# GLA q and k projections of heads 2 and 3: q with tokens stationary, k in two token halves

## Chip, cores and metric

The kernel runs on one core of a Trainium2 chip. The metric is device microseconds (us) of one execution, and lower is better. The core has a matrix engine (TensorE, "PE" in the profile, with its weight loads as "PEld"), three engines for elementwise work (VectorE "DVE", ScalarE "ACT", GpSimd "POOL") and SyncE ("SP"), which here only issues DMAs. Every engine works through its own instruction list in order and waits where an operand is not ready.

## The reference

One layer of a hybrid decoder for 320 tokens: 256 of a prompt and 8 sequences of 8 sample tokens, all with the same weights. What matters here is the input projection and the GLA branch:

```python
h = _rmsnorm(x, norm_mix_w)
proj = h @ _f32(w_in)
mq, mk, mv, mo, mi, mf, gq, gk, gv, gr, gal, gate_a, gate_b = jnp.split(proj, split_at, axis=-1)
...
q_g = gq.reshape(B, T, G_HEADS, G_DK) * (G_DK ** -0.5)
k_g = gk.reshape(B, T, G_HEADS, G_DK)
...
o_g, S1 = _gla(q_g, k_g, v_g, log_a, _f32(S0))
```

`G_HEADS` is 4 and `G_DK` is 128, so q and k of one GLA head are 128 columns of `w_in` each; `D_MODEL`, the length of the contraction, is 2048. An mLSTM branch of four heads, a merge with gates and a ConvFFN follow.

## The kernel before

**Precision and layout.** Each float32 product is made of three matmuls in a reduced float32 format (`F32R`): the weight is split into a high and a low part (`wh`, `wl`), the normalized input as well (`hH[k]`, `hL[k]` for the 16 blocks `k` of 128 of the contraction), and `mm3` (L75 to L78) adds high x high, high x low and low x high into one accumulator. In `mm3` a 128x128 block of weights is stationary and all 320 tokens move, so the result stands with output columns on partitions and tokens along the free axis.

**Weights.** `weights` (L63 to L73) loads 512 KB into a tile `raw`, rounds it on ACT into `wh` (L71) and subtracts on DVE into `wl` (L72). `raw` has four buffers; `wh` and `wl` have three each. A buffer of `wh` or `wl` is free again when the last matmul that reads it is done, so at most three chunks of weights are split ahead of PE or held by it.

**Projections.** `product` (L89) accumulates 256 output columns in two PSUM tiles `big` (96 matmuls). `proj2` uses it for v, and for q, k and v of the mLSTM heads. `proj1` (L442) makes 128 columns in one `big` tile with 48 matmuls, and is used for q and k of GLA heads 2 and 3, whose columns are projected when those heads come up (heads 0 and 1 are done at the start). PSUM is two pools of four banks, `big` and `mx`; the small matmuls of the heads use `mx`.

**Heads.** The loop over `h` at L789 issues for each head: q and k (heads 2 and 3), v, `gla_head`, then q, k and v of the mLSTM head and `mlstm_head`. Both head functions are long chains of small steps over PE, DVE, ACT and POOL. They share the tiles `vH`, `vL`, `vs` (the split values), so a head's chain starts when the chain before it has used them. Their recurrent states lie in a pool of three buffers with the tag `state`, handed out in turn: `S0` of the GLA head (L581), then two tiles `C0` of the mLSTM head (L701). A buffer can be written again when the stores of its last user (L695 for `S0`, L787 for `C0`) have landed.

**Order of work.** The program is written head by head, and a scheduler moves each engine's instructions so that the chains of a head lie between the dense projection matmuls of what comes next. What it decides is fixed in each engine's list before the run. The chain of GLA head 1 thus lies, on PE, among the projections of head 2.

Lines that the prediction's steps touch, in the order of a GLA head: levels of the attention matrix (L626, L634, L643), split of it (L507, L508, L496, L498), numerators (L513, L500), norm (L528 to L539), transposes (L543), `hn` (L545, L546), decayed keys (L658 to L664), transposes (L669, L670), their split (L673, L674, L558, L560), masked keys `km` (L684), state update (L689 on PE, L693 on DVE), store of the state (L695). Of the mLSTM head: values (L476, L466, L483, L480), product with the state (L574), scores (L755 to L757), numerators (L513 again).

Of the kernel before, what the change touches and what calls it, by code (L numbers as in the profile page):

```python
# [10 lines left out]
F32 = mybir.dt.float32  # L11
F32R = mybir.dt.float32r
U8 = mybir.dt.uint8
AF = mybir.ActivationFunctionType
ALU = mybir.AluOpType
PSUM = bass.MemoryType.PSUM

P = 128
DM = 2048
NK = DM // P  # L20
T = 256
B = 8
S = 8
NS = B * S
N = T + NS
H = 4
DH = 256
DK = 128
DV = 256
# [8 lines left out]
C_GQ, C_GK, C_GV, C_GR = 4104, 4616, 5128, 6152  # L38
# [5 lines left out]
def step_kernel(ctx: ExitStack, tc: tile.TileContext, a: dict):  # L44
    nc = tc.nc
    cp = ctx.enter_context(tc.tile_pool(name="cp", bufs=1))
# [4 lines left out]
    def big():  # L51
        return ps.tile([P, 512], F32, tag="big", name="big")

    def mx(name="mx"):
        return ps.tile([P, 512], F32, tag="mx", name=name)
# [4 lines left out]
    w_in = a["w_in"][0]  # L60


    def weights(src, kc, mc, halves=1):  # L63

        raw = ring.tile([P, kc, mc * P], F32, tag="raw", name="raw", bufs=RAW)
        nc.sync.dma_start(raw, src.rearrange("(k p) c -> p k c", p=P))
        hi = ring.tile([P, kc, mc * P], F32R, tag="wh", name="wh", bufs=3)
        lo = ring.tile([P, kc, mc * P], F32R, tag="wl", name="wl", bufs=3)
        for i in range(halves):
            ks = slice(i * kc // halves, (i + 1) * kc // halves)  # L70
            nc.scalar.activation(hi[:, ks], raw[:, ks], AF.Copy)  # L71
            nc.vector.tensor_tensor(lo[:, ks], raw[:, ks], hi[:, ks].bitcast(F32), op=ALU.subtract)  # L72
        return hi, lo  # L73

    def mm3(out, wh, wl, xh, xl, first, last):  # L75
        nc.tensor.matmul(out, wh, xh, start=first, stop=False)  # L76
        nc.tensor.matmul(out, wh, xl, start=False, stop=False)  # L77
        nc.tensor.matmul(out, wl, xh, start=False, stop=last)  # L78
# [18 lines left out]
    ident = cp.tile([P, P], F32, name="ident")  # L97
# [20 lines left out]
    rstd_bc = cp.tile([P, N], F32, name="rstd_bc")  # L118
# [1 line left out]

    dram = ctx.enter_context(tc.tile_pool(name="dram", bufs=1, space=bass.MemoryType.DRAM))
    xT_d = [dram.tile([P, 4, N], F32, name=f"xTd{c}") for c in range(4)]
    hH = [cp.tile([P, N], F32R, name=f"hH{k}") for k in range(NK)]
    hL = [cp.tile([P, N], F32R, name=f"hL{k}") for k in range(NK)]

    def pool(name, bufs, side=None):
        p = tc.tile_pool(name=name, bufs=bufs, side=side, reuse_waits="tile")
# [4 lines left out]
    def evac_scaled(dst, pt, scale):  # L132
        nc.vector.scalar_tensor_tensor(dst, pt[:, :N], scale, rstd_bc, op0=ALU.mult, op1=ALU.mult)


    with tc.tile_pool(name="st", bufs=1) as st:
# [67 lines left out]
        gq, gk = (mg.tile([P, 2, N], F32, tag=t, name=t) for t in ("gq", "gk"))  # L204
# [32 lines left out]
    with tc.tile_pool(name="mc", bufs=1, reuse_waits="tile") as mc, \  # L237
            tc.tile_pool(name="wk", bufs=2, reuse_waits="tile") as wk:
        def w320(name):
            return wk.tile([P, N], F32, tag="w320", name=name, bufs=8)  # L240
# [87 lines left out]
        for k0 in range(0, NK, 8):  # L328
            raw = graw[:, k0:k0 + 8]
            hi = ring.tile([P, 8, P], F32R, tag="wh", name="wh", bufs=3)  # L330
            lo = ring.tile([P, 8, P], F32R, tag="wl", name="wl", bufs=3)
            nc.gpsimd.memset(hi.bitcast(F32), 0.0)
            nc.gpsimd.memset(lo.bitcast(F32), 0.0)
            for r, d, n in ((0, 0, 4), (4, 32, 4), (8, 64, 16)):
                nc.scalar.activation(hi[:, :, d:d + n], raw[:, :, r:r + n], AF.Copy)
                nc.vector.tensor_tensor(lo[:, :, d:d + n], raw[:, :, r:r + n], hi[:, :, d:d + n].bitcast(F32),
                                        op=ALU.subtract)
            for kk in range(8):
                k = k0 + kk
# [96 lines left out]
        def proj2(tag, c0, scale):  # L436
            t = (wk if tag == "v" else mg).tile([P, 2, N], F32, tag=tag, name=tag, bufs=1)
            for m, pt in enumerate(product(w_in, c0, DM, hH, hL)):
                evac_scaled(t[:, m], pt, scale)
            return t  # L440

        def proj1(dst, c0, scale):  # L442
            pt = big()
            for k0 in (0, 8):
                hi, lo = weights(w_in[k0 * P:(k0 + 8) * P, c0:c0 + P], 8, 1)
                for kk in range(8):
                    k = k0 + kk
                    mm3(pt[:, :N], hi[:, kk], lo[:, kk], hH[k], hL[k], k == 0, k == NK - 1)
            evac_scaled(dst, pt, scale)

# [336 lines left out]
        for h in range(H):  # L789
            if h == 2:  # L790
                gq, gk = (mg.tile([P, 2, N], F32, tag=t, name=t) for t in ("gq", "gk"))
            if h >= 2:
                proj1(gq[:, h % 2], C_GQ + 128 * h, DK ** -0.5)
                proj1(gk[:, h % 2], C_GK + 128 * h, 1.0)
            gv = proj2("v", C_GV + 256 * h, 1.0)
            gla_head(h, gq[:, h % 2], gk[:, h % 2], gv)
            mq = proj2("q", C_MQ + 256 * h, 1.0)
            mk = proj2("k", C_MK + 256 * h, DH ** -0.5)
            mv = proj2("v", C_MV + 256 * h, 1.0)
            mlstm_head(h, mq, mk, mv)  # L800
# [22 lines left out]
    for br, c0 in ((1, C_GR), (0, C_MO)):  # L823
        for j in range(4):
            for m, pt in enumerate(product(w_in, c0 + 256 * j, DM, hH, hL)):
                i = br * 8 + 2 * j + m
# [43 lines left out]
    for j in range(8):  # L870
        for m, pt in enumerate(product(wo, 256 * j, DM, mH, mL)):
            k = 2 * j + m
# [3 lines left out]
                                           op0=ALU.mult, op1=ALU.subtract)  # L876
# [16 lines left out]
    with tc.tile_pool(name="c0", bufs=2, side="right", reuse_waits="tile") as c0p:  # L893
        for i in range(6):
# [3 lines left out]
            pt = mx("mx26")  # L898
# [13 lines left out]
    for p0 in range(0, NF, 8):  # L912
        pn = min(8, NF - p0)
        aH, aL = [], []
        for c0 in range(p0, p0 + pn, 2):
# [19 lines left out]
            for m, pt in enumerate(product(wg, c0 * P, DM, hH, hL)):  # L935
# [5 lines left out]
                                        op=ALU.mult)  # L941
# [5 lines left out]
        if p0 + pn == NF:  # L947

            cv = conv1.rearrange("p r c -> p (r c)")
            for i in range(7):  # L950
                r0, rn = i * P, min(P, 18 * NF - i * P)
                pt = mx("mx29")
# [8 lines left out]
        for j in range(8):  # L961
            for m, pt in enumerate(product(wd[p0 * P:(p0 + pn) * P], 256 * j, pn * P, aH, aL)):
                k = 2 * j + m
# [7 lines left out]
                elif k >= 14:  # L971
                    for src in (sacc, sq) if k == 14 else (sq,):
                        for jj in (0, 1, 2) if k == 14 else (2, 1, 0):
                            t0, tn = TOK[jj]
                            nc.tensor.matmul(pf[:tn, jj:jj + 1], src[:, t0:t0 + tn], ones[:, 0:1],
                                             start=(src is sacc and jj == 0), stop=(k == 15 and jj == 0))
                y = tmp("y")
                nc.scalar.activation(y, x2[k], AF.Copy, scale=fnw[:, k:k + 1])
                pt = mx("mx28")
# [9 lines left out]
    for jj, (t0, tn) in enumerate(TOK):  # L989
        for hf in range(4):  # L990
# [5 lines left out]
            dst = a["o_y_p"][0, t0:t0 + tn, cs] if jj < 2 else ysv[:, cs]  # L996
# [34 lines left out]
```

## Time and profile before

| | us |
|---|---|
| median of 2 runs (1915.26 and 1915.6) | 1915.43 |
| span of the profiled execution, first to last instruction | 1912.6 |
| what lies around the span, taken as the difference | 2.8 |
| PE busy | 1896.9 |
| DVE busy | 1084.1 |
| ACT busy | 773.0 |
| POOL busy | 339.0 |

The views read below are: the page's busy times, the table by stretches of time (`A:B` from the span's start, its length, then for each engine its busy time and, after x, its instructions, the granted clock of PE, the mean share of the DMA engines and GB/s), the groups of instructions by line, the list of who waited for whom, and the timeline (start, duration, engine, line, operation, tile written and tiles read, shapes, count; in brackets the idle time of the engine before it). Consecutive equal instructions are merged in the timeline, and the duration then runs from the first start to the last end. Matmuls overlap in the pipeline, so the step from one start to the next is their cost, not the duration of one. "SPq" is SyncE's DMA queue, L12 a line of the kernel.

### The profile page before, as it was taken

What the parts mean: (1) busy time and instruction counts of PE and PEld (TensorE: products, weight loads), DVE (VectorE), ACT (ScalarE), POOL (GpSimd) and SP (SyncE); (2) the same over time, 40 slices, a digit from 0 to 9 for tenths busy, and PEclk for the clock granted to TensorE, in tenths of its full rate; (3) what the DMA queues carried; (4) which work ended last, traced back from release to release, by engine and by line L of the source; (5) the groups of instructions that cost most, each with busy time, mean ns of one, the idle gap of its engine ahead of it and who ended that gap; (6) DMA issues with size and microseconds to landing.
All of it is one profiled execution on the core that took longest, in us unless ns stands there. A gap on an engine that the chain in (4) does not pass through costs nothing.

```text
span 1912.6 us, 32523 instructions
## 1 busy us (share of the span) xinstructions
PE 1896.9 (99%) x13123; PEld 1879.8 (98%) x13123; DVE 1084.1 (57%) x1672; ACT 773.0 (40%) x1102; POOL 339.0 (18%) x614
## 2 busy tenths in 40 slices
PE   9999999999999999999999999999999999999997
PEld 8999999999999999999999999999999999999997
DVE  5778686877544444446555545545554554555455
ACT  5544443454433333333344333433433443343345
POOL 4334241522000000021112102101110210111014
PEclk9999999999999999999999999999999999999998
DMA  8656676756545555565454454444444454444442
GB/s 239 203 149 196 189 220 185 225 171 216 167 146 153 148 150 154 146 188 168 151 151 146 152 153 146 154 147 152 150 148 155 144 154 148 150 153 146 154 148 93
DMA packets 300192, 311.03 MB, mean 163 GB/s; under 512 B 15268, under 2 KB 292026, under 8 KB 300041
## 3 DMA queue, kind: packets, MB, share of 16 engines
q1 hardware_dynamic: 287849, 283.53, 49.2%
q0 software_dynamic: 7296, 23.90, 3.6%
q8 instruction: 103, 1.69, 0.4%
q10 hardware_dynamic: 4896, 1.52, 0.3%
q14 instruction: 48, 0.39, 0.1%
HBM read 286.44 MB, written 22.47 MB: 162 GB/s over the span
## 4 chain that ended last, share of the span: by engine, by line


## 5 line engine op out<-in xcount | busy, mean ns | idle before, releaser
L72 DVE TENSOR_TENSOR wl<-raw,wh 128x1024 fp32r<-128x1024 f32 (+1 forms) x510 | 629.1, 1235 | 607.5 <-ACT wh L71 606.9
L71 ACT ACTIVATE wh<-raw 128x1024 fp32r<-128x1024 f32 (+1 forms) x510 | 534.9, 1050 | 879.5 <-PE big L77 736.1
L77 PE MATMUL big<-hL,wh 128*128 128x320 f32 x2832 | 878.5, 310 | 0.0
L76 PE MATMUL big<-hH,wh 128*128 128x320 f32 x2832 | 878.3, 310 | 0.0
L78 PE MATMUL big<-hH,wl 128*128 128x320 f32 x2832 | 877.7, 310 | 0.0
L76 PEld LDWEIGHTS big<-hH,wh 128*128 128x128 f32 x2832 | 532.2, 188 | 1.8 <-issue 1.2
L77 PEld LDWEIGHTS big<-hL,wh 128*128 128x128 f32 x2832 | 532.2, 188 | 1.0 <-issue 0.4
L78 PEld LDWEIGHTS big<-hH,wl 128*128 128x128 f32 x2832 | 532.3, 188 | 0.7
L77 PE MATMUL big<-aL,wh 128*128 128x320 f32 x704 | 217.9, 310 | 0.0
L78 PE MATMUL big<-aH,wl 128*128 128x320 f32 x704 | 217.6, 309 | 0.0
L76 PE MATMUL big<-aH,wh 128*128 128x320 f32 x704 | 215.8, 309 | 0.0
L78 PEld LDWEIGHTS big<-aH,wl 128*128 128x128 f32 x704 | 132.4, 188 | 0.0
L77 PEld LDWEIGHTS big<-aL,wh 128*128 128x128 f32 x704 | 132.4, 188 | 0.0
L76 PEld LDWEIGHTS big<-aH,wh 128*128 128x128 f32 x704 | 131.8, 188 | 0.0
L926 POOL COPY conv<-u 128x2 f32<-128x2 f32 x44 | 8.3, 188 | 527.4 <-DVE u L923 527.4
L857 POOL TENSOR_TENSOR g<-g 128x320 f32<-128x320 f32 x16 | 14.8, 924 | 366.4 <-DVE g L853 366.4
L77 PE MATMUL big<-mL,wh 128*128 128x320 f32 x256 | 78.8, 309 | 0.0
L76 PE MATMUL big<-mH,wh 128*128 128x320 f32 x256 | 78.7, 309 | 0.0
L78 PE MATMUL big<-mH,wl 128*128 128x320 f32 x256 | 78.7, 309 | 0.0
L964 DVE TENSOR_TENSOR x<-big,x 128x320 f32<-128x320 f32 x96 | 46.6, 488 | 46.4 <-PE big L78 46.4
L938 POOL TENSOR_TENSOR g<-g,uc 128x256 f32<-128x256 f32 x44 | 32.6, 741 | 211.9 <-DVE g L937 211.9
L77 PE MATMUL big<-yL,wh 128*128 128x320 f32 x192 | 59.2, 308 | 0.0
(394 smaller groups left out, 1791.9 us busy)
## 6 DMA issues: line engine op xcount, KB each, us to landing
raw<-in_w_in SPq DMA_DIRECT2D x176, 512.0 KB, 3.8
raw<-in_ffn_w_up SPq DMA_DIRECT2D x88, 512.0 KB, 3.6
raw<-in_ffn_w_gate SPq DMA_DIRECT2D x88, 512.0 KB, 3.5
raw<-in_ffn_w_down SPq DMA_DIRECT2D x88, 512.0 KB, 3.4
raw<-in_w_out SPq DMA_DIRECT2D x32, 512.0 KB, 3.7
C<-in_state_mlstm_C SPq DMA_DIRECT2D x32, 256.0 KB, 5.9
o_C_s<-C POOLq DMA_DIRECT2D x32, 256.0 KB, 4.8
raw<-in_w_branch_a SPq DMA_DIRECT2D x16, 512.0 KB, 3.5
```

The costliest lines, as they stand in the source:

```text
L71: nc.scalar.activation(hi[:, ks], raw[:, ks], AF.Copy)
L72: nc.vector.tensor_tensor(lo[:, ks], raw[:, ks], hi[:, ks].bitcast(F32), op=ALU.subtract)
L76: nc.tensor.matmul(out, wh, xh, start=first, stop=False)
L77: nc.tensor.matmul(out, wh, xl, start=False, stop=False)
L78: nc.tensor.matmul(out, wl, xh, start=False, stop=last)
L857: nc.gpsimd.tensor_tensor(sg[m], sg[m], acc[m], op=ALU.add)
L926: nc.gpsimd.tensor_copy(conv1[:, 0:2, c], u[:, T:T + 2])
L938: nc.gpsimd.tensor_tensor(g[:, 0:T], g[:, 0:T], gel[m][:, 0:T], op=ALU.mult)
L964: nc.vector.tensor_tensor(x2[k], pt[:, :N], x2[k], op=ALU.add)
```

## The change

For heads 2 and 3, `proj1` is replaced by two functions.

`proj_tokens` makes q of both heads at once (256 columns). A block of 128 tokens of `hH` or `hL` is stationary and 256 weight columns move. The 256 prompt tokens go into one PSUM tile `po`. The 64 sample tokens use the tile `hS`, which holds their high and low parts side by side (filled by 16 copies on POOL, in a buffer of the pool `state`), and go into a second PSUM tile `pS`, as does high x low weight with 64 stationary columns. The result stands with tokens on partitions, and six transposes with an add turn it round.

`proj_halves` makes k of one head with 128 weight columns stationary. The tokens go in two halves of 160. For one half, the high and the low part of the input move side by side (320 columns) against the high weights; then 160 columns of the high part move against the low weights. The two parts are added at the end. For this `hH[k]` and `hL[k]` become the halves of one tile `hP[k]`.

```diff
-    hH = [cp.tile([P, N], F32R, name=f"hH{k}") for k in range(NK)]
-    hL = [cp.tile([P, N], F32R, name=f"hL{k}") for k in range(NK)]
+    hP = [cp.tile([P, 2, N], F32R, name=f"hP{k}") for k in range(NK)]
+    hH, hL = [t[:, 0] for t in hP], [t[:, 1] for t in hP]
...
-        def proj1(dst, c0, scale):
-            pt = big()
+        def proj_halves(dst, c0, scale):
+
+            halves = [slice(n * 160, (n + 1) * 160) for n in range(2)]
+            out = [big(), big()]
             for k0 in (0, 8):
                 hi, lo = weights(w_in[k0 * P:(k0 + 8) * P, c0:c0 + P], 8, 1)
                 for kk in range(8):
                     k = k0 + kk
-                    mm3(pt[:, :N], hi[:, kk], lo[:, kk], hH[k], hL[k], k == 0, k == NK - 1)
-            evac_scaled(dst, pt, scale)
+                    for n, ns in enumerate(halves):
+                        pair = out[n][:, 0:N].rearrange("p (x t) -> p x t", x=2)
+                        nc.tensor.matmul(pair, hi[:, kk], hP[k][:, :, ns], start=(k == 0), stop=False)
+                        nc.tensor.matmul(pair[:, 0], lo[:, kk], hH[k][:, ns], start=False, stop=(k == NK - 1))
+            whole = w320("whole")
+            for n, ns in enumerate(halves):
+                nc.scalar.copy(whole[:, ns], out[n][:, 160:320])
+                nc.vector.tensor_tensor(whole[:, ns], out[n][:, 0:160], whole[:, ns], op=ALU.add)
+            nc.vector.scalar_tensor_tensor(dst, whole, scale, rstd_bc, op0=ALU.mult, op1=ALU.mult)
+
+        def proj_tokens(dst, c0, scale):
+
+            po, pS = big(), big()
+            hS = wk.tile([P, B, DV + 4], F32R, tag="state", name="hS", bufs=3)
+            hS = [hS[:, k // 2, P * (k % 2):P * (k % 2) + P] for k in range(NK)]
+            for k in range(NK):
+                nc.gpsimd.tensor_copy(hS[k].rearrange("p (x t) -> p x t", x=2), hP[k][:, :, T:N].bitcast(F32))
+            for k0 in range(0, NK, 4):
+                hi, lo = weights(w_in[k0 * P:(k0 + 4) * P, c0:c0 + 256], 4, 2)
+                for t in range(2):
+                    ts = slice(t * P, (t + 1) * P)
+                    for kk in range(4):
+                        k = k0 + kk
+                        for i, (x, w) in enumerate(((hH, hi), (hL, hi), (hH, lo))):
+                            nc.tensor.matmul(po[:, t * 256:(t + 1) * 256], x[k][:, ts], w[:, kk],
+                                             start=(k == 0 and t == 0 and i == 0),
+                                             stop=(k == NK - 1 and t == 1 and i == 2))
+                for kk in range(4):
+                    k = k0 + kk
+                    if k:
+                        nc.tensor.matmul(pS[0:64, 0:256], hH[k][:, T:N], lo[:, kk], start=False, stop=False)
+                    nc.tensor.matmul(pS[:, 0:256], hS[k], hi[:, kk], start=(k == 0), stop=(k == NK - 1))
+                    if k == 0:
+                        nc.tensor.matmul(pS[0:64, 0:256], hH[k][:, T:N], lo[:, kk], start=False, stop=False)
+            nat = wk.tile([P, 512], F32, tag="AT", name="nat")
+            nc.scalar.copy(nat, po)
+            ns = w320("ns")[:, 0:256]
+            nc.vector.tensor_copy(ns, pS[:, 0:256])
+            for m in range(2):
+                pt = mx("mx7")
+                for t in range(2):
+                    nc.tensor.transpose(pt[:, t * P:(t + 1) * P], nat[:, t * 256 + m * P:t * 256 + (m + 1) * P], ident)
+                nc.tensor.transpose(pt[:, T:T + P], ns[:, m * P:(m + 1) * P], ident)
+                nc.vector.tensor_copy(dst[:, m], pt[:, 0:N])
+                nc.vector.tensor_tensor(dst[:, m, T:N], dst[:, m, T:N], pt[:, N:N + 64], op=ALU.add)
+                nc.vector.scalar_tensor_tensor(dst[:, m], dst[:, m], scale, rstd_bc, op0=ALU.mult, op1=ALU.mult)
...
         for h in range(H):
             if h == 2:
                 gq, gk = (mg.tile([P, 2, N], F32, tag=t, name=t) for t in ("gq", "gk"))
+                proj_tokens(gq, C_GQ + 256, DK ** -0.5)
             if h >= 2:
-                proj1(gq[:, h % 2], C_GQ + 128 * h, DK ** -0.5)
-                proj1(gk[:, h % 2], C_GK + 128 * h, 1.0)
+                proj_halves(gk[:, h % 2], C_GK + 128 * h, 1.0)
```

The change also moves instructions, since the scheduler orders every engine anew. Three places matter below. In the rows that follow, a name's number tells one tile from another (`S0_1994` before and `S0_1978` now are both the state of GLA head 1), and the lines of the changed kernel stand 46 higher than the same lines before.

On PE, in the chain of GLA head 1, at its transposes of the normed output (L543 before, L589 now). Before:

```order
L76 MATMUL big_2999<-hH9_112,wh_3063 128x320
L77 MATMUL big_2999<-hL9_128,wh_3063 128x320
L78 MATMUL big_2999<-hH9_112,wl_3064 128x320
L543 MATMUL mx9_2171<-ident_67,hs_2167 128x128
L543 MATMUL mx9_2179<-ident_67,hs_2167 128x128
L543 MATMUL mx9_2171<-ident_67,hs_2167 128x128 x2
L543 MATMUL mx9_2179<-ident_67,hs_2167 128x128 x2
L76 MATMUL big_2999<-hH10_113,wh_3063 128x320
L77 MATMUL big_2999<-hL10_129,wh_3063 128x320
L78 MATMUL big_2999<-hH10_113,wl_3064 128x320
```

Now:

```order
L546 MATMUL mxi_2108<-vs_845,asp_841 128x256 x2
L589 MATMUL mx9_2155<-ident_67,hs_2151 128x128
L589 MATMUL mx9_2163<-ident_67,hs_2151 128x128
L589 MATMUL mx9_2155<-ident_67,hs_2151 128x128 x2
L589 MATMUL mx9_2163<-ident_67,hs_2151 128x128 x2
L715 MATMUL mx14_2180<-ident_67,kd_2171 128x128
L716 MATMUL mx14_2180<-ident_67,kr_2176 128x128
```

Before, projection matmuls (`big`) stand on both sides of the transposes; now the chain's own steps follow each other. This holds for the whole stretch whose two ends are the second place.

On PE, at the two ends of that stretch. The last projection matmuls ahead of it, with the third chunk of q's weights (`wh_2955`, `wl_2956`), in the changed kernel:

```order
L474 MATMUL big_2858<-wh_2955,hP11_114 128x256
L620 MATMUL mxi_2108<-S0_1978,qz_612 32x256 x8
L474 MATMUL big_2858<-wl_2956,hP11_114 128x256
L680 MATMUL mx12_2083<-lv_z_2077 128x64
L680 MATMUL mx12_2097<-lv_z_2091 128x64
L689 MATMUL mx12_2083<-lv_z_2077 64x32
L689 MATMUL mx12_2097<-lv_z_2091 64x32
```

and the first ones behind it:

```order
L803 MATMUL mx18_2705<-qH_2642,kL_2645 128x128
L481 MATMUL big_2859<-wh_2879,hS_2860 128x256
L483 MATMUL big_2859<-wl_2880,hP0_103 64x256
L480 MATMUL big_2859<-wl_2880,hP1_104 64x256
L481 MATMUL big_2859<-wh_2879,hS_2860 128x256
L480 MATMUL big_2859<-wl_2880,hP2_105 64x256
L481 MATMUL big_2859<-wh_2879,hS_2860 128x256
```

Between L689 of the first of these fences and L481 of the second, PE's list has no row that writes a `big` tile. The matmuls that read `hS` with the first chunk of weights (`wh_2879`) stand behind the whole rest of GLA head 1 and behind the scores of mLSTM head 1 (L803). Until they are done, three chunks of q's weights are held: `wh_2879`, `wh_2917`, `wh_2955`.

On POOL, at the store of the state of GLA head 1. Before:

```order
L717 DMA bc_3795<-rows_575 128x456
L695 DMA o_S_s<-S0_1994 128x8x256
L595 TENSOR_TENSOR pr_3145<-gq_2872,gk_2873 128x320
L596 TENSOR_TENSOR pr_3145<-gq_2872,gk_2873 128x160
L531 TENSOR_TENSOR sc_2767<-sc_2767,mhalf_80 128x3
```

Now:

```order
L763 DMA bc_3928<-rows_559 128x456
L741 DMA o_S_s<-S0_1978 128x8x256
L466 CAST hS_2860<-hP0_103 128x128
L466 CAST hS_2860<-hP1_104 128x128
L466 CAST hS_2860<-hP2_105 128x128
```

The copies into `hS` follow the store directly. In the pool `state` the tiles come in the order `S0` of head 1, `C0_2603`, `C0_2608`, `hS_2860`, `S0_3256` (head 2), so with three buffers in turn `hS` takes the buffer of that `S0`, and `S0` of head 2 the one of `C0_2603`.

On SP, in the changed kernel, behind the last chunk of v of head 2:

```order
L66 DMA raw_3194<-in_w_in 128x4x256
L66 DMA raw_3224<-in_w_in 128x4x256
L628 DMA S0_3256<-in_state_gla_S 128x8x256
L66 DMA raw_3509<-in_w_in 128x4x256
L66 DMA raw_3539<-in_w_in 128x4x256
```

The load of head 2's state stands ahead of the first chunk for the mLSTM q of head 2 (`raw_3509`); before, it stood two products later, between the second and the third chunk of the mLSTM v of head 2, and its buffer was that of `S0` of head 1.

## Prediction

> **What bounds the kernel now.** I read the busy times first, then a table by stretches of time, then the page's groups with what ended the idle time before them.
>
> ```profile
> PE 1896.9 (99%) x13123; PEld 1879.8 (98%) x13123; DVE 1084.1 (57%) x1672; ACT 773.0 (40%) x1102; POOL 339.0 (18%) x614
> ...
> 480.00:800.00 320.00, 320.00 (x2185) 320.00 (x2184) 150.32 (x176) 117.81 (x143) 10.56 (x12) 1.00 0.52 152
> ...
> L71 ACT ACTIVATE wh<-raw 128x1024 fp32r<-128x1024 f32 (+1 forms) x510 | 534.9, 1050 | 879.5 <-PE big L77 736.1
> ```
>
> PE is the bound: 1896.9 of the 1912.6 us of the span. In a stretch of projections alone, 2185 matmuls with 320 moving columns take 320 us, so one costs 0.1465 us. The third row shows the ring of split weights running full: ACT waits for PE to free a buffer of `wh`, 736.1 us in all. PE is never short of weights, and the chains of the heads lie between the dense matmuls at no cost but their own PE time. Two things can therefore move the end: how long PE's own work takes, and whether PE must wait with no dense work ready.
>
> **Direct cost of the new matmuls.** Prices of the forms that the change adds:
>
> ```profile
> 146.25 0.64 PE L689 MATMUL mx<-vs,km 128*128 128x256 f32 x4
> 146.73 0.31 PE L77 MATMUL big<-hL,wh 128*128 128x320 f32 x1
> ...
> 157.71 0.19 PEld L755 LDWEIGHTS mx<-qL,kH 128*128 128x128 f32 x1
> ...
> 158.06 0.19 PEld L755 LDWEIGHTS mx<-qH,kL 128*128 128x128 f32 x1
> ...
> 222.14 0.82 PE L543 MATMUL mx<-ident,hs 128*128 128x128 f32 x6
> ```
>
> Four matmuls with 256 moving columns take 146.73 - 146.25 = 0.48 us, 0.12 each. Six transposes take 0.82 us for starts and one duration of 0.27, so 0.11 each. Between the two rows of PEld lie three weight loads with matmuls of 256, 64 and 128 columns: 0.35 us, 0.115 per load, though the two short matmuls have hardly anything to stream. So a matmul that streams quickly still pays about 0.115 for the load of its successor.
>
> - q: removed are 96 matmuls at 0.1465, 14.06 us. Added are 96 for `po` and 32 for `pS`, all with 256 moving columns: 128 x 0.12 = 15.36. With six transposes (0.66) that is +2.0.
> - k, per head: 48 x 0.1465 = 7.03 become 32 x 0.1465 + 32 with 160 columns. By columns alone (0.1465 and 0.12 at 320 and 256 give 0.41 ns a column) these would cost 0.08 each, by the load 0.115. I take 0.115: 4.69 + 3.68 = 8.37, +1.34, for two heads +2.7.
>
> Sum +4.7. Lower bound: 160 columns at 0.08, so k +0.4 for both heads and +2.4 in all. Upper bound: the step of L757, which I cannot separate from its neighbours, could be 0.19 for 160 columns, k +7.5; with 0.1 more for each of the 16 matmuls of 64 stationary columns and its successor, +12. The copies and adds behind the accumulators go to DVE and ACT, which are busy 57% and 40%, while `big` has four banks; they cost nothing while PE has other matmuls ready. DMA bytes are the same.
>
> **The stall.** The order of the changed kernel holds the larger term. `hS` takes the buffer of the state of GLA head 1, so its copies must wait until that state has been updated, stored and landed. PE's list puts the matmuls that read `hS` behind the rest of GLA head 1 and the scores of mLSTM head 1; until four of them are done, all three `wh` buffers hold q's chunks, and no dense matmul can be ready. PE then runs at the pace of a chain that is now hidden. First, what work PE has until then:
>
> ```profile
> 194.44 0.38 PE L629 MATMUL mx<-lv_z 128*128 128x128 f32 x2
> ...
> 194.44:251.14 56.70, 56.70 (x437) 54.63 (x436) 40.83 (x92) 22.66 (x41) 9.38 (x15) 1.00 0.64 195
> ```
>
> In PE's list q of head 2 begins next to this L629, before and now. From there to the end of mLSTM head 1's scores PE is busy for all of 56.7 us. 288 dense matmuls lie in it (q, k, v of GLA head 2 and the mLSTM q: 48 + 48 + 96 + 96), 42.2 us; the chain's own PE work is the rest, 14.5. Now only 72 dense matmuls lie there (three chunks of q, 8.6 us), then the chain, then 13 matmuls of `pS` with 11 of mLSTM head 1's numerators ahead of the fourth chunk (24 x 0.12 = 2.9): 26.0 us of work. Whatever passes beyond that is stall.
>
> When does the chain let PE go? Its rows before, from the last level on:
>
> ```profile
> 211.89 0.42 PE L643 MATMUL mx<-lv_z 128*64 128x32 f32 x4
> 213.04 0.88 DVE L498 TENSOR_TENSOR asp<-AT,asp 32x32 fp32r<-32x32 f32 x4 [0.30 <-ACT asp L496]
> 216.05 0.28 PE L500 MATMUL mxi<-vs,asp 128*128 128x256 f32 x1
> 218.81 0.82 ACT L537 ACTIVATE hs<-mx,sc 128x256 f32<-128x256 f32 x2
> 222.41 1.23 DVE L72 TENSOR_TENSOR wl<-raw,wh 128x1024 fp32r<-128x1024 f32 x1 [2.25 <-ACT wh L71]
> 225.06 0.22 DVE L659 TENSOR_TENSOR kd<-gb 128x64 f32<-128x64 f32 x1
> 226.46 0.46 ACT L661 ACTIVATE kd<-kd 128x320 f32<-128x320 f32 x1
> 227.73 0.42 DVE L662 TENSOR_TENSOR kd<-kd,gk 128x256 f32<-128x256 f32 x1
> 228.07 0.42 DVE L664 TENSOR_TENSOR kr<-kd,gk 128x256 f32<-128x256 f32 x1
> 231.16 0.27 PE L669 MATMUL mx<-ident,kd 128*128 128x128 f32 x1
> 234.14 1.30 DVE L684 TENSOR_TENSOR km<-ks,bm 128x512 fp32r<-128x512 f32 x2
> 237.76 0.64 PE L689 MATMUL mx<-vs,km 128*128 128x256 f32 x4
> 238.99 1.22 DVE L72 TENSOR_TENSOR wl<-raw,wh 128x1024 fp32r<-128x1024 f32 x1
> 242.85 0.91 POOL L695 DMA_DIRECT2D o_S_s<-S  x1 [4.50 <-DVE dec L730]
> 248.54 0.37 SPq L582 DMA_DIRECT2D S<-in_state_gla_S  x1
> ```
>
> The last two rows show the release: the store goes out at 242.85 and the next user of the buffer (then head 2's load) starts 5.7 us later. From the end of L643 (212.3) to there are 36.2 us, and much of it is waiting in queues behind dense work that will not be there: L500 2.1 us after `asp`, L543 2.5 after L537's end (219.63), `hn` 0.6 (DVE's L72 at 222.41), L661 1.2, L662 0.8, L669 2.7 after L664's end, L689 2.9 after the first `km` (half of 1.30), the state update 1.1 (L72 at 238.99). Sum 13.9, less 0.5 for a step of mLSTM head 1 that now stands ahead of `km` on DVE: 13.4. The chain alone thus needs 22.8 us. It starts when PE has done its 72 matmuls and the level steps between them: 194.4 + 8.6 + 4.2 (twelve of L634, each two instructions at 0.115: 2.8; the product with S, half of the 1.95 of L574 in the next rows: 1.0; L629 and L643 0.4) = 207.2. So `hS` may be written from 230.0. Then four copies on POOL:
>
> ```profile
> L474 POOL COPY vr<-v 128x256 f32<-128x256 f32 x16 | 9.9, 646 | 4.3 <-DVE gw L380 3.0 <-DVE br L375 1.4
> ...
> L293 POOL CAST lvl<-lvl_f 128x64 uint8<-128x64 f32 x7 | 1.7, 237 | 0.0
> ...
> 244.18 0.69 DVE L483 TENSOR_TENSOR vs<-mx,vs 64x512 fp32r<-64x512 f32 x1
> 246.10 0.68 DVE L480 TENSOR_TENSOR vL<-mx,vH 128x512 fp32r<-128x512 f32 x1
> 247.00 1.95 PE L574 MATMUL mxi<-C,qz 128*32 128x258 f32 x32
> 248.88 0.39 PE L755 MATMUL mx<-qH,kH 128*128 128x256 f32 x1
> ...
> 250.84 0.30 PE L757 MATMUL mx<-qH,kL 128*128 128x128 f32 x1
> ```
>
> between 0.24 (128x64) and 0.65 (128x256) each, I take 0.37: 231.5. On PE the mLSTM steps stand ahead of it: L574 (1.95) and the scores (248.88 to 251.1, 2.2). They need the values of mLSTM head 1, which DVE splits in 0.69 + 0.68 us right behind the state update (224.3), and end at about 229.8. With 0.8 for the first matmuls of `pS` and 1.05 for a split of weights on ACT (the mean of L71 above), dense work resumes at 233.4 at full clock. The clock is not granted through gaps:
>
> ```profile
> 6.00:9.46 3.46, 2.52 (x14) 1.58 (x14) 2.49 (x7) 2.85 (x8) 2.42 (x10) 1.00 1.07 297
> 9.46:12.87 3.41, 3.41 (x13) 2.92 (x14) 3.41 (x9) 2.40 (x8) 0.00 (x0) 0.50 1.08 317
> ```
>
> After a stretch with 2.5 of 3.5 us busy, PE got half its clock for 3.4 us. If that happens in the last part, L574 and the scores end at 233.9, `pS` takes 1.6, and `hS` is no longer what comes last: 236.6. I take the middle, 235.0, and 1.7 for dense work that restarts at half clock (half of 3.4).
>
> Stall: 235.0 - 194.4 - 26.0 = 14.6. With 1.7 and 4.7, +21.0 us. The span of 1912.6 becomes 1933.6; the median lies 2.8 above the span, so **1936.4 us**, 1.1% above 1915.43. Bounds of the stall: 10 if the chain's steps overlap by 3 us more than the rows show, 28 if all 13.4 us of waits stay.
>
> The Trainium skill, page "TensorE: Matmul & The Clock Gate", section "Part 1: The HAM clock gate (the "warmup" mystery)", says that the clock falls to half after a whole idle window of about 3.4 us. The rows above differ: PE had no such gap in 6.00:9.46, and the clock fell; the measurement decides. By the page alone no gap here would be long enough for certain, and the sum would be about 3 us less.
>
> **Rivals.**
>
> 1. *No stall.* The chain is done before PE's list reaches it, and only the direct cost is left: 1920. For it speaks that PE never waits for a chain now; against it that three chunks of q are 8.6 us of cover, used up before a chain of 22.8 begins.
> 2. *The chain keeps its length.* If its steps are slow for another reason than the queues, the 13.4 us stay: 1950. For it: some waits in the rows are named only by what came last. Against it: each ends just as a dense instruction of its engine ends.
> 3. *Half clock throughout.* If the whole stretch from 207 on runs at half clock and each resumption too, the PE steps on the chain (L574 2.0, scores 2.2, L543 0.8, the rest about 2) double: 1936.4 + 7 = 1943.
> 4. *SP's queue, slower by over 2%.* The load of head 2's state stands on SP ahead of the mLSTM q's weights and waits for the stores of `C0_2603`:
>
> ```profile
> 255.88 0.28 PE L513 MATMUL mx<-vH,AH 128*128 128x258 f32 x1
> ...
> 281.15 0.88 SPq L703 DMA_DIRECT2D C<-in_state_mlstm_C  x2
> ...
> 289.85 1.39 SPq L703 DMA_DIRECT2D C<-in_state_mlstm_C  x3
> ...
> 194.00:204.00 10.00, 10.00 (x75) 10.00 (x74) 7.86 (x23) 3.80 (x6) 4.33 (x6) 1.00 1.03 340
> ```
>
> From the numerators of mLSTM head 1 to the release of that buffer took 25.3 us (281.15), of the second 34.0. Now the numerators come at about 234: the load goes out at 259, weights behind it are split by about 265. PE has 33 us of work from 235 (the rest of q, k, v, and the end of mLSTM head 1), until 268. It decides from 3 us later than that. If the load waits 34.0 us (268), and its 1 MB and the 2 MB of `C0` behind it hold back the weights for 9 at the 340 GB/s that the last row shows with the DMA engines full, the weights are ready at about 283 instead of 268. PE waits 15 us more, restarts cold a second time with up to 3.4, and the time is about 1955.
>
> **Chances.** Forecast 0.57, no stall 0.05, chain keeps its length 0.15, half clock 0.14, SP's queue 0.08; 0.01 is left for a gain that I cannot name, as no term here is negative. A measurement of this kernel can tell about 2% from no change: the limits are 1877 and 1954. Rival 4 and the tail of rival 2 give 0.10 for slower, the rest is within 2%. The low end 1925 lies at the lower bounds (stall 10, no cold restart, direct 2.4: 1928) with some way towards rival 1; the high end 1956 takes in rivals 2, 3 and 4.
>
> **What would show it.** In the changed profile: a stretch at about 205 to 237 us with few `big` matmuls, PE's waits put down to the chain's engines and to POOL's copies into `hS`; the store of S of head 1 at about 224 instead of 242.85, and the first copy 5.7 us behind it; the granted clock at 0.5 there; ACT and DVE without weight splits for that time; 160-column matmuls at a step of 0.115. It is wrong if dense matmuls of k or v stand in that stretch, if PE is as busy as before and yet later (direct cost), or if a second gap opens near 265.

## The result and the profile after

| | before | after |
|---|---|---|
| median, us | 1915.43 | 1936.88 (runs of 1935.04 and 1938.71) |
| span of the profiled execution | 1912.6 | 1936.9 |
| PE busy | 1896.9 | 1910.7 |

The ratio is 1.0112, 95% interval 1.0082 to 1.0141: slower by 1.1%, which is within 2%. The forecast was 1936.4. In us the change costs 21.4; since the two runs lie 3.7 us apart, the interval is wide, 15.7 to 27.0.

Two rows of the page of the changed kernel, busy times and the ring of split weights:

```profile
PE 1910.7 (99%) x13193; PEld 1890.1 (98%) x13193; DVE 1090.6 (56%) x1681; ACT 769.7 (40%) x1103; POOL 336.7 (17%) x630
...
L71 ACT ACTIVATE wh<-raw 128x1024 fp32r<-128x1024 f32 (+1 forms) x510 | 534.8, 1050 | 867.7 <-PE big L77 715.3
```

PE is still 99% busy, so the page alone says little: 13.8 us more of PE work and 10.5 us more outside it (span less busy, 26.2 against 15.7). The first dense matmuls behind the heads (`yH`) begin at 548.4 us instead of 524.0 (before, then after; behind the count: shortest, median and longest duration in ns, then first and last start in the stretch from 400 to 700):

```profile
L76 PE MATMUL big<-yH,wh x112: 306/308/309, 524.0 to 699.5; 128*128 128x320 f32 x112
L76 PE MATMUL big<-yH,wh x89: 306/308/309, 548.4 to 699.7; 128*128 128x320 f32 x89
```

The traces are 24.4 us apart there, and the spans differ by 24.3 (the profiled execution of the changed kernel is the longer of its two, 1938.71, so this is more than 21.4). Everything is lost before that, and the table by stretches of the changed kernel shows where:

```profile
207.00:212.00 5.00, 3.92 (x36) 2.71 (x28) 2.40 (x10) 2.75 (x11) 0.00 (x0) 1.00 0.00 0
212.00:217.00 5.00, 1.54 (x6) 1.07 (x6) 2.38 (x8) 1.19 (x3) 2.03 (x3) 0.64 0.00 0
217.00:222.00 5.00, 3.05 (x10) 2.06 (x10) 4.08 (x13) 1.26 (x4) 0.99 (x3) 0.50 0.16 66
222.00:227.00 5.00, 4.33 (x19) 4.17 (x20) 4.80 (x12) 1.66 (x4) 1.09 (x2) 0.50 0.25 75
227.00:232.00 5.00, 4.58 (x55) 3.40 (x55) 4.61 (x10) 1.81 (x5) 0.91 (x1) 0.99 0.60 206
232.00:237.00 5.00, 2.90 (x15) 2.76 (x15) 2.55 (x8) 1.32 (x5) 3.19 (x13) 0.69 0.02 7
237.00:242.00 5.00, 5.00 (x40) 4.74 (x40) 2.95 (x7) 3.77 (x11) 0.93 (x4) 0.97 0.22 62
```

Before, PE was busy for every one of these microseconds (56.70 of 56.70 us in the prediction's row 194.44:251.14). Now it stands idle for 9.7 of the first 30, and the granted clock (third from the end of a row) falls to 0.5. The DMA share behind it (0.00 at 207 to 217) says the same from the other side: no weights are loaded, because no buffer for them is free. The list of waits names the links of the chain one by one:

```profile
PE mx L715 <- DVE kd L708: 2.5, 1, 2.5
PE mx L589 <- ACT hs L583: 2.3, 1, 2.3
PE big L481 <- POOL hS L466: 2.1, 1, 2.1
PE mx L680 <- POOL lv_z L672: 1.8, 2, 1.2
PE mx L735 <- DVE km L730: 1.3, 1, 1.3
```

L680's wait lies in GLA head 0, before 119 us, and stood in the profile before as well (as L634, 1.8); the other four are new. The timeline of the chain:

```profile
195.82 0.38 PE L675 MATMUL mx<-lv_z 128*128 128x128 f32 x2
...
208.56 0.70 PE L689 MATMUL mx<-lv_z 128*64 128x32 f32 x4
...
213.74 1.54 PE L589 MATMUL mx<-ident,hs 128*128 128x128 f32 x6 [2.31 <-ACT hs L583]
...
217.79 0.47 PE L715 MATMUL mx<-ident,kd 128*128 128x128 f32 x1 [2.51 <-DVE kd L708]
...
222.68 2.05 PE L735 MATMUL mx<-vs,km 128*128 128x256 f32 x8 [1.30 <-DVE km L730]
...
227.13 0.91 POOL L741 DMA_DIRECT2D o_S_s<-S  x1 [2.71 <-DVE S L739]
...
233.81 4.11 POOL L466 CAST hS<-hP 128x128 fp32r<-128x128 f32 x16 [5.78 <-DMA o_S_s<-S]
...
234.41 0.58 PE L481 MATMUL big<-wh,hS 128*128 128x256 f32 x1 [2.10 <-POOL hS L466]
...
237.39 1.06 ACT L71 ACTIVATE wh<-raw 128x1024 fp32r<-128x1024 f32 x1 [2.90 <-PE big L481]
...
238.65 0.40 PE L474 MATMUL big<-wh,hP 128*128 128x256 f32 x2
```

The order of events is the one that the prediction gave: the level steps end, the chain runs alone, the state is stored, the copies into `hS` follow the landing of that store, PE takes `hS`, the first `wh` buffer comes free, ACT splits, dense work resumes. The first row is the old L629, 1.38 us later than before, although of the change only the tiles `hP` and one matmul of q stand ahead of it. What makes this offset stays open; in the kernels below the same step lies 0.7 to 2.5 us later than before. Less this offset, dense work resumes at 237.3.

### The profile page after: what moved, and what is told of

Read it like the earlier page. It is cut to its first block, busy times and chain, and to the rows that moved or that the text cites. A ratio compares the mean times of both kernels' runs of the same rounds, so it can differ in the third digit from the quotient of the medians.

```text
span 1936.9 us, 32680 instructions
## 1 busy us (share of the span) xinstructions
PE 1910.7 (99%) x13193; PEld 1890.1 (98%) x13193; DVE 1090.6 (56%) x1681; ACT 769.7 (40%) x1103; POOL 336.7 (17%) x630
## 4 chain that ended last, share of the span: by engine, by line
## 5 line engine op out<-in xcount | busy, mean ns | idle before, releaser
L76 PE MATMUL big<-hP,wh 128*128 128x320 f32 x2768 | 858.7, 310 | 0.2 <-ACT wh L71 0.2
L77 PE MATMUL big<-hP,wh 128*128 128x320 f32 x2768 | 858.5, 310 | 0.0
L78 PE MATMUL big<-hP,wl 128*128 128x320 f32 x2768 | 858.0, 310 | 0.0
L77 PEld LDWEIGHTS big<-hP,wh 128*128 128x128 f32 x2768 | 520.5, 188 | 1.8 <-issue 1.2
L76 PEld LDWEIGHTS big<-hP,wh 128*128 128x128 f32 x2768 | 520.5, 188 | 0.8 <-ACT wh L71 0.3
L78 PEld LDWEIGHTS big<-hP,wl 128*128 128x128 f32 x2768 | 520.2, 188 | 0.5
L77 PE MATMUL big<-aL,wh 128*128 128x320 f32 x704 | 217.9, 310 | 0.0
```

## Experiments

Three theories. **A**: PE waits for buffers that new tiles take from the chain of GLA head 1, and only about 4.7 us are the price of the new matmuls. In its first form, A1, as the prediction has it, `hS` alone is that lock. In a second, A2, the staging tiles `nat`, `ns` (q) and `whole` (k) are another, since they take buffers (`AT`, `w320`) that the chains use, and until they are filled the PSUM tiles `big` behind them are not free. **B**: the loss is the price of the matmuls. **C**: the chain itself became longer. Differences are to the kernel before, measured beside each kernel.

### All new tiles in buffers of their own (e6_all_own)

The pool `tmps` has eight buffers that nothing uses while the heads run.

```diff
-            whole = w320("whole")
+            whole = tmp("whole")
...
-            hS = wk.tile([P, B, DV + 4], F32R, tag="state", name="hS", bufs=3)
-            hS = [hS[:, k // 2, P * (k % 2):P * (k % 2) + P] for k in range(NK)]
+            hS = [tmps.tile([P, N], F32R, tag="tmp", name="hS") for _ in range(8)]
+            hS = [hS[k // 2][:, P * (k % 2):P * (k % 2) + P] for k in range(NK)]
...
-            nat = wk.tile([P, 512], F32, tag="AT", name="nat")
-            nc.scalar.copy(nat, po)
-            ns = w320("ns")[:, 0:256]
+            nat = [tmp("nat")[:, 0:256] for _ in range(2)]
+            for t in range(2):
+                nc.scalar.copy(nat[t], po[:, t * 256:(t + 1) * 256])
+            ns = tmp("ns")[:, 0:256]
...
```

> The whole change, but hS and the three staging tiles (nat, ns, whole) take buffers of the pool tmps that nothing uses in the head phase. Theory A (the loss is PE waiting for the buffers that hS and the staging tiles take from the head chain): the stretch near 207 to 238 us is filled with dense matmuls again, only the direct cost of +4.7 (2.4 to 12) is left, about 1920 (1918 to 1927). Rival B (the loss is the price of the new matmuls, and PE would be as late without any wait): about 1936, as the changed kernel. Rival C (the chain's steps themselves became longer, whatever the buffers): the stretch stays, 1933 or more.

Measured: 1920.76, +4.8 (ratio 1.0026, 1.0016 to 1.0036). The same stretches in its trace:

```profile
212.00:217.00 5.00, 5.00 (x43) 4.83 (x42) 2.31 (x7) 3.11 (x11) 0.00 (x0) 1.00 0.35 108
...
222.00:227.00 5.00, 5.00 (x41) 5.00 (x40) 3.50 (x9) 1.75 (x4) 1.92 (x4) 1.00 0.52 170
...
232.00:237.00 5.00, 5.00 (x37) 5.00 (x37) 3.32 (x6) 2.09 (x4) 0.00 (x0) 1.00 0.47 130
```

No gap, full clock, with all of the change's matmuls in place. B and C fall: 16.6 of the 21.4 us go with the buffers, as PE's waits and as the half clock that came with them.

### Only hS free (e1_own_buffer), only the staging tiles free (e7_staging_own)

The first takes only the lines on `hS` of the diff above, the second only the others.

> Only hS has buffers of its own; nat, ns and whole stay where the change puts them. Theory A1 (the buffer of hS alone holds PE, as the prediction says): about 1920, and dense matmuls in the stretch from 207 to 238. Theory A2 (the staging tiles are a second lock: nat waits for AT buffers of the head chain, so the accumulator banks of q and k are not freed): now q and all of k of head 2 are done as cover (a little over 20 us of PE work instead of 8.6), then a stall again in the later part of the chain, about 99 small matmuls without a dense one: 1923 to 1934. Rival B (price of the matmuls): 1936.

> The other half: nat, ns and whole have buffers of their own, hS stays in the state buffer. Theory A1 and A2 agree: hS comes first in PE's list and holds the ring of weights, so the stretch stays as in the changed kernel, 1936 (1933 to 1938). If instead the staging tiles alone are the lock, about 1920.

Measured: 1937.49 (+21.6, ratio 1.0112, 1.0097 to 1.0127) and 1937.08 (+21.1, the same ratio and interval). Freeing `hS` alone gives nothing, and so does freeing the rest alone. A1 falls as the whole story: either of the two locks costs the full price. With `hS` free I had expected 1923 to 1934 under A2; the 1937.49 are more, and by themselves would fit B, which only the kernel with all buffers free rules out. What the second looks like, by stretches, by tiles and, at the copies, by time in the kernel with `hS` free:

```profile
222.00:227.00 5.00, 5.00 (x42) 5.00 (x41) 2.85 (x8) 1.51 (x3) 0.56 (x1) 1.00 0.50 155
227.00:232.00 5.00, 1.85 (x11) 1.08 (x10) 3.56 (x12) 2.07 (x4) 1.35 (x4) 1.00 0.54 188
...
247.00:252.00 5.00, 0.89 (x5) 0.59 (x4) 1.31 (x6) 2.59 (x10) 0.88 (x1) 0.50 0.59 198
```

```profile
L453 PE MATMUL big<-hP,wl x32: 235/237/321, 218.2 to 227.0; 128*128 128x160 f32 x32
L481 PE MATMUL big<-wh,hS x16: 277/280/363, 200.5 to 217.9; 128*128 128x256 f32 x16
```

```profile
253.78 0.37 ACT L814 COPY co<-mx 128x256 f32<-128x256 f32 x1 [1.70 <-PE mx L600]
```

```profile
L485 ACT COPY nat<-big x1: 604/604/604, 254.1 to 254.1; 128x512 f32<-128x512 f32 x1
```

```profile
L456 ACT COPY whole<-big x2: 323/330/336, 254.6 to 254.8; 128x160 f32<-128x160 f32 x2
```

q is done at 217.9 and k at 227.0, and PE is full until then. But `nat` and `whole` are written only at 254.1 and 254.6. For 27 us all four banks of `big` hold finished products, and PE idles for 10.4 of the 25 us from 227 to 252 (five such stretches added). In this trace no copy is seen to wait for its buffer: ACT takes them right behind a copy of mLSTM head 1 (L814), and in PE's list the first matmul of v (256.07) stands behind the steps of that chain too. The scheduler laid down these lists for the buffers that it had. That the shared buffers are why the copies stand there follows from the kernel with all buffers free, not from a wait in this one.

### Which staging tile (e12_whole_own, e11_nat_own, e2_k_only)

In all three `hS` is out of the way. The first frees `whole` as well, the second `nat` and `ns` as well. The third has no q tiles at all:

```diff
-                proj_tokens(gq, C_GQ + 256, DK ** -0.5)
             if h >= 2:
+                proj1(gq[:, h % 2], C_GQ + 128 * h, DK ** -0.5)
                 proj_halves(gk[:, h % 2], C_GK + 128 * h, 1.0)
```

> The whole change; hS and whole have buffers of their own, nat and ns stay where the change puts them. It splits the second lock. Theory A3 (all four big banks must be held at once: po and pS by nat and ns, the two halves of k by whole; with whole free, k gives its two banks back and v can be projected): no stretch without dense matmuls, direct cost only, about 1920.8. Theory A2 in its narrower form (nat's wait for an AT buffer is a lock by itself): a stall as with hS alone freed, 1930 to 1937.

> Only k is changed, and whole stays in the buffers that the change gives it (w320), no tile of q is there. Theory A3: k's two banks alone can be held while two others go on, so between the price of k alone (about 1918.5) and some us more: in the order of the instructions 46 and 18 matmuls of the chain follow one another with four dense ones between, near the scores of mLSTM head 1. I expect 1920 to 1926. If w320 holds nothing up, as fast as with buffers of its own; if it is a full lock, 1930 or more.

> The other half of the split: hS, nat and ns have buffers of their own, whole stays in w320. Theory A3 (four big banks must be held at once): q gives its two banks back, k's two are held, v's two follow and then wait behind the tile v that the chain of head 1 still reads, so a smaller stall than with hS alone freed, as in the run with k alone, which lost 6.8 us to the same tile: direct cost 4.8 plus 3 to 9, 1923 to 1930. In the order of the instructions the stretch of 99 chain matmuls near head 1 is gone, and one of 50 stands in GLA head 2. If whole alone were the second lock, about 1937 as with hS alone freed.

Measured: 1922.76 (+7.0, ratio 1.0036, 1.0023 to 1.005), 1926.57 (+10.8, 1.0059, 1.0043 to 1.0074) and 1930.37 (+15.0, 1.0077, 1.006 to 1.0094). The copies of the first:

```profile
L485 ACT COPY nat<-big x1: 610/610/610, 270.6 to 270.6; 128x512 f32<-128x512 f32 x1
```

```profile
L456 ACT COPY whole<-big x4: 283/292/292, 225.5 to 311.5; 128x160 f32<-128x160 f32 x4
```

`nat` is even later here, 270.6 against q's end at 216.4, and its two banks stand still for 54 us. It hardly matters: k's first half is copied at 225.5, and v and the next products go through the two banks that are left. PE takes the first of them as soon as k's sum has been read from it:

```profile
226.25 0.41 PE L76 MATMUL big<-hP,wh 128*128 128x320 f32 x1 [0.48 <-DVE whole L457]
```

The time is 2.0 above the 1920.8 that I expected, but its interval (+4.4 to +9.6) overlaps that of the kernel with all buffers free (+3.1 to +6.9). So `nat` and `ns` alone are not the second lock; it closes when all four banks are held (A3 of the expectations). In the kernel with k alone (the next row) and in the one with `nat` and `ns` free (the two rows behind it) the two banks of `whole` are held, those of q are not:

```profile
220.00:240.00 20.00, 16.89 (x112) 16.35 (x111) 15.79 (x37) 7.66 (x14) 4.01 (x6) 0.90 0.53 162
```

```profile
320.00:340.00 20.00, 15.28 (x89) 13.73 (x87) 14.73 (x36) 7.96 (x15) 4.03 (x8) 0.83 0.39 123
```

```profile
L456 ACT COPY whole<-big x4: 292/312/326, 265.9 to 361.4; 128x160 f32<-128x160 f32 x4
```

PE idles for 3.1 us in GLA head 1 of the one, and for 4.7 in head 2 of the other, where k of head 3 was done at 310.6 and the last copy into `whole` starts at 361.4. In GLA head 1 of the latter the same two banks are held from 225.8 to 265.9 as well, and PE idles for only 0.2 us there: how much two held banks cost differs from head to head. The 1926.57 and the 1930.37 are 0.6 and 0.4 beyond the upper ends of what I expected, and I have not taken them apart. The middle size of the losses fits the four banks better than a single tile with the price of a full lock; that is argued from sizes and not shown by a wait.

### k ahead of q (e4_k_first)

```diff
+                proj_halves(gk[:, 0], C_GK + 256, 1.0)
                 proj_tokens(gq, C_GQ + 256, DK ** -0.5)
-            if h >= 2:
-                proj_halves(gk[:, h % 2], C_GK + 128 * h, 1.0)
+            if h == 3:
+                proj_halves(gk[:, 1], C_GK + 384, 1.0)
```

> The change with one thing in another order: k of head 2 is projected ahead of q of heads 2 and 3. The matmuls of k (32 x 0.1465 + 32 x 0.115 = 8.4 us by the prediction's prices) then stand ahead of the lock as more cover. Theory A: the stall shrinks by about 8, so 1927 to 1930. Rival B: no change, 1936. Rival C (the chain starts later by as much as it has more cover, since PE's list holds the chain's steps behind the dense work): between 1930 and 1936.

Measured: 1934.66 (+18.7, ratio 1.01, 1.0084 to 1.0117), 2.7 less than the change's +21.4, where I expected 8; the two intervals overlap, so even the 2.7 is not clear of noise. The links of the chain:

```profile
219.00 1.02 PE L589 MATMUL mx<-ident,hs 128*128 128x128 f32 x6 [0.23 <-ACT hs L583]
...
237.13 4.37 POOL L466 CAST hS<-hP 128x128 fp32r<-128x128 f32 x16 [4.15 <-DMA o_S_s<-S]
```

The transposes L589 come 5.3 us later than in the changed kernel (213.74), and the copies into `hS` 3.3 later (233.81). The time lies where the expectation's rival C put it (1930 to 1936): the 8.4 us of k's matmuls stand ahead of most of the chain and delay it, so little of them is gained as cover. The rest is not taken apart. In this kernel k's two banks are held from 205.5 until the copies into `whole` at 250.9, and PE waits another 1.5 us at 248.9, so the second lock may have had a part.

### The price of each part (e8_k_only_own, e9_q_only_own)

k alone with `whole` in `tmps`, and q alone with `hS`, `nat` and `ns` in `tmps`.

> Only k is changed (two halves of 160), q is projected as before, and the staging tile whole has buffers that nothing else uses: the price of k alone. By the prediction's prices 2 x (32 x 0.1465 + 32 x 0.115 - 48 x 0.1465) = +2.7, about 1918.6. If a 160-column matmul costs by its columns alone, +0.8 (1916.7); if each takes the 0.19 of the upper bound, +7.5 (1923). In the trace of the changed kernel a pair of 320 and 160 columns took 0.255 to 0.26 us, which gives 2 x (32 x 0.2575 - 7.03) = +2.4.

> Only q is changed (tokens stationary), k is projected as before, and hS, nat and ns have buffers that nothing else uses: the price of q alone. By the prediction 128 x 0.12 + 6 x 0.11 - 96 x 0.1465 = +2.0, about 1917.9. If the 16 matmuls with 64 stationary columns cost more than the others (the 0.1 of the upper bound for each and its successor), +5, about 1921. Together with the k of the other run it should give the +4.8 that the whole change cost with all buffers its own.

Measured: 1919.77 (+4.0, ratio 1.0019, 1.001 to 1.0028) and 1918.08 (+2.3, 1.0013, 1.0004 to 1.0021); in neither trace does PE wait in the heads beyond what it waited before (1.8 us in GLA head 0, and 0.2). The steps of k in the first (starts are what counts), and of q's sample matmuls in the kernel with k first:

```profile
205.46 0.35 PE L452 MATMUL big<-hP,wh 128*128 128x320 f32 x1
205.65 0.24 PE L453 MATMUL big<-hP,wl 128*128 128x160 f32 x1
205.72 0.34 PE L452 MATMUL big<-hP,wh 128*128 128x320 f32 x1
```

```profile
246.43 0.28 PE L481 MATMUL big<-wh,hS 128*128 128x256 f32 x1
246.55 0.28 PE L480 MATMUL big<-wl,hP 128*64 128x256 f32 x1
246.67 0.28 PE L481 MATMUL big<-wh,hS 128*128 128x256 f32 x1
```

A pair of 320 and 160 columns takes 0.26 us, against 0.22 by columns. A matmul with 64 stationary columns takes the 0.12 of the others, so the 0.1 more that the prediction's upper bound gave them falls away. The two prices add up to 6.3 where the whole change cost 4.8 with its buffers free; the intervals (1.9 to 5.4, 0.8 to 4.0, 3.1 to 6.9) allow both. Both parts cost time and neither saves any, so even with no wait left the change is no gain: k moves as many columns as before (32 x 320 + 32 x 160 = 48 x 320) in more instructions, q moves more (128 x 256 against 96 x 320).

## Why the prediction was right, step by step

- **Direct cost, +4.7.** With all buffers free +4.8 (3.1 to 6.9 by the interval). q was put at +2.0 and measured +2.3 (0.8 to 4.0), k at +2.7 and +4.0 (1.9 to 5.4). The mean of 0.1465 and 0.115, 0.131 a matmul, stands beside 0.13 in the rows (half of 0.26). The terms of the upper bound add up to 12.7, not 12; nothing came near it.
- **Stall and cold restart, 14.6 + 1.7 = 16.3.** The changed kernel less the one with all buffers free: 21.4 - 4.8 = 16.6. The parts came out differently. Dense work resumed at 237.3 by the clock of the profile before, not at 235.0, and without a cold start: PE's clock is 0.97 in 237:242. The 2.3 us that the first was short and the 1.7 of the second nearly cancel, and that the forecast met the median within 0.5 us is luck in this: the 16.6 are only about 10 us of PE standing idle (9.7 in the table above), the rest, by the estimate under "Half clock" below, mostly slow work at that clock, which the prediction had put at 3.3 (1.6 in the stall, 1.7 behind it). With two runs 3.7 us apart, the 16.6 themselves are known to some us only.
- **The chain alone, 22.8.** From the end of L689 to the first copy are 24.5 us. The chain took 36.2 us before, so most of the 13.4 us of queue waits that I had taken off are gone, and rival 2 fell (1950). The store went out at 227.13, not at 224. What was too short is the release, 6.7 us from store to copy instead of 5.7, and PE's own steps at half clock.
- **Half clock.** I had it set in only in the last part, and took half its price there. It came with the first gap:

```profile
213.40:227.10 13.70, 9.02 (x36) 7.41 (x37) 10.90 (x31) 4.01 (x10) 3.21 (x6) 0.50 0.15 51
227.10:233.90 6.80, 4.79 (x56) 3.47 (x54) 6.04 (x13) 2.50 (x8) 0.99 (x2) 1.00 0.46 157
233.90:237.30 3.40, 2.89 (x13) 2.89 (x14) 1.12 (x5) 0.54 (x3) 3.40 (x14) 0.50 0.00 0
```

  In 17.1 us at half clock PE was busy for 11.9; at full clock that would have been up to 6 us less, an estimate from these rows alone, which no run has taken apart. Rival 3 thus happened in part: the eight matmuls of L735 took 2.05 us, where four took 0.64 before, and L589 1.54 instead of 0.82. Between the two stretches the clock was full, and L620 and the scores ran at their old pace. `hS` was what came last all the same (PE's wait of 2.10 ends with POOL's copies); I take it that the half clock had delayed the chain before it as much.
- **The copies, 0.37 each.** 16 copies take 4.11 us, 0.26 each. PE took the first 0.6 us after it began.
- **SP's queue, rival 4.** It fell, and its premise with it. The load of head 2's state went out at 246.38, not at 259, 7 us ahead of the first store of `C0` of mLSTM head 1 (253.74), so it cannot have waited for that buffer; it follows the last matmul that reads `hS` (245.91) by 0.5 us. By these times the pool gave it the buffer of `hS`, not the one that a turn of three would give.

```profile
245.91 0.32 PE L481 MATMUL big<-wh,hS 128*128 128x256 f32 x1
...
246.38 0.45 SPq L628 DMA_DIRECT2D S<-in_state_gla_S  x1
```

- **What the prediction missed.** "Until four of them are done, all three `wh` buffers hold q's chunks" is right for this kernel, and enough for the whole stall, as the run with the staging tiles free shows. But it is not the only lock. Had it been, rival 1's 1920 would have been the time with `hS` moved, and that kernel takes 1937.49. The order of the changed kernel could not show the second lock, since the first one stands ahead of it; the tags of `nat` and `whole` in the diff could.

## What to carry to other kernels

Before a new tile goes into a shared pool, look up who holds its buffer until when, and what the operation that waits for it holds in turn: here a staging tile held PSUM banks, and 16 copies held three buffers of weights. When a freed wait gives nothing, look for a second one behind it before giving up the theory: here each of two locks cost the full price, and only the kernel that freed both showed it. Dense work covers a chain between its links, as in the kernel before; put ahead of it on an engine that works in order, it delays the chain: 8.4 us of k's matmuls ahead of it gained some 2.7 here, not clear of noise.

## What the runs showed of the hardware

In the changed kernel the clock fell to half with no wait of PE above 2.5 us. The Trainium skill, page "TensorE: Matmul & The Clock Gate", section "Part 1: The HAM clock gate (the "warmup" mystery)", asks for a whole idle window of about 3.4 us. The rows above differ: the first fall, at 213.4, came in a wait of 2.31, and the second came after 6.8 us in which PE was busy for 4.79, behind a wait of 2.1. At half clock the matmuls with 256 moving columns are 0.21 us apart instead of 0.12:

```profile
234.79 0.41 PE L483 MATMUL big<-wl,hP 128*64 128x256 f32 x1
235.01 0.41 PE L480 MATMUL big<-wl,hP 128*64 128x256 f32 x1
235.22 0.41 PE L481 MATMUL big<-wh,hS 128*128 128x256 f32 x1
```
